# A hybrid encoder in fp32 halves: another simulation behind the scheduler's order

## The chip, the cores and the metric

The kernel runs on one core of one Trainium2 chip. The metric is the device time of one execution in microseconds (us), as the median of three runs. A profile of one further execution gives the instructions of each engine with their times. The engines are TensorE (PE in the profile, with its weight loads as PEld), VectorE (DVE), ScalarE (ACT), GpSimd (POOL) and SyncE (SP, which here only issues transfers).

## What is computed

Two layers of a bidirectional encoder over 512 tokens and 16 learned meta tokens (528 rows of 1024 channels). Each layer adds half a gated feed-forward block, a mixer of two parallel branches, and half a second feed-forward block:

```python
def reference(x, meta_tokens, norm_gains, ...):
    h = jnp.concatenate([meta, x], axis=1)
    for l in range(DEPTH):                      # DEPTH = 2
        h = h + 0.5 * swiglu(rmsnorm(h, norm_gains[l, 0]), ffn_w_gate[l, 0], ffn_w_up[l, 0], ffn_w_down[l, 0])
        h = h + mixer(rmsnorm(h, norm_gains[l, 1]), w_in[l], ...)
        h = h + 0.5 * swiglu(rmsnorm(h, norm_gains[l, 2]), ffn_w_gate[l, 1], ffn_w_up[l, 1], ffn_w_down[l, 1])
    return rmsnorm(h, final_norm)[:, N_META:]
```

The mixer projects to queries, keys, values and gates of both branches. Branch A is gated linear attention in both directions (4 heads), computed by chunks with a state carried from chunk to chunk. Branch B is softmax attention with 8 query heads and 2 key heads, normalised and rotated queries and keys. The branches are multiplied by sigmoid gates, added and projected back.

## The kernel before, in words

Channels lie on the 128 partitions and tokens along the free dimension; `h` is 8 chunks of 128 x 528. Every large product is made of three matmuls on halves: an operand is split into a high part `hi` (a cast, on ScalarE) and a low part `lo` (the difference, on VectorE), and hi*hi, hi*lo and lo*hi are summed in PSUM.

**Weights.** The class `Weights` goes through a plan (`PLAN`) of slabs of 128 x 1024. A slab is fetched by SyncE's queue (L168 and L203), cast to `whi` on ScalarE (L222) and subtracted to `wlo` on VectorE (L223), or on GpSimd while the gates are projected. `whi` and `wlo` have four buffers each and the raw slabs three. `use` makes slabs 4 places ahead (`AHEAD_MADE`) and fetches 6 ahead (`AHEAD_FETCHED`). The gate and up matrices of the feed-forward blocks are multiplied with seven products of sums of sub-blocks in place of eight; some of those sums of weights are formed by transfers that add into their target, issued on GpSimd's queue (L178), with a negated copy on ScalarE (L173) before them.

**Feed-forward blocks** (`ffn`). For each of 11 pairs of columns there are seven products (L498) of 24 matmuls; between them ScalarE copies partial results out of PSUM (`snap`, L504) and VectorE adds (L511, L516, L520, L531, L537). After each of three groups the down projection (`product`, L378) runs and is added to `h` (L465, L474). The last down product leads into the next norm: squares (L412), their sum (L416), the mean over channels as a matmul (`means`, L384), and the operands of the next stage (`Norm.pair`, L422 to L442, tiles `xc`, or `Norm.operand`, tiles `x`).

**Mixers** (`mixer`). Projections of x (`project`, L378 on the tiles `mm`) alternate in program order with the linear attention of two pairs of heads (`gla_pair`, L586 to L735: decays, transposes at L651, states at L687, scores inside a block at L714, outputs at L723 and L724) and with softmax attention (`attention`, L748 to L902: scores at L832 and L833, transposes of the probabilities at L857 and L867, weighted values at L874 and L875). One unit of attention is two blocks of 128 queries of one head; the probabilities of the next unit are made before the weighted values of this one. Four of the 16 gate projections come before attention in program order and twelve after it; none of them depends on attention.

**What sets the order.** The kernel is written in a framework that records instructions in program order, with their dependences and buffers, and orders them itself when the context is closed. For that it plays the program on a simulated machine: an engine of that machine is given, among the instructions whose inputs and buffers are ready in simulated time, the one of the highest priority. Priority is program order, except that `tc.high_priority()` raises what is recorded inside it (the mean of a norm in `Norm.rs`, the copies out of PSUM in `project`, the query norms in attention). `tc.issue_after` fixes an instruction behind another on the same engine. The result is one fixed stream per engine, DMA issues of SyncE, ScalarE and GpSimd among them, with waits on semaphores where another engine's work is needed. On the chip each engine executes its stream in that order, whatever is ready. By default the simulated machine is a simple one, which gives an engine its next instruction when the last one is over and starts each transfer after a fixed latency.

The diff touches only the line that opens the context, L1085 in `kernel`:

## Time and profile before

| what | us |
|---|---|
| median of 3 runs | 2314.39 (2314.13 to 2316.66) |
| the profiled execution | 2324.93 |
| its span, first to last instruction | 2323.2 |
| TensorE busy | 2244.2 |
| VectorE busy | 1525.0 |
| ScalarE busy | 1192.3 |
| GpSimd busy | 231.8 |

The mean clock granted to TensorE in the profiled execution is 0.983 of full speed. In the profile a row such as "PE ss L384 <- DVE t L416" says that PE's instruction of line 384, which writes the tile `ss`, stood still until VectorE's instruction of line 416 was over. L12 is line 12 of the kernel; a line can be that of a helper which many callers share, as L378 is. A wait for several things is put down to the last of them. A PE that is busy need not be at its peak: the records of matmuls overlap.

The stages follow each other in time as follows: first feed-forward block 0 to 400 us, mixer of layer 0 to 824, second feed-forward block to 1182, the first block of layer 1 to 1555, its mixer to 1961, the last block and the final norm to the end. In layer 1, from the mixer on, only the 512 tokens without the meta tokens are carried.

### The profile page before, as it was taken

The numbers are of one execution on the slowest core, as the hardware profiler recorded it, in microseconds if no ns is written. First come the engines' busy times: TensorE is split into PE (matmuls) and PEld (weight loads), VectorE is DVE, ScalarE is ACT, GpSimd is POOL, SyncE is SP. The second block draws the span as 40 slices with busy tenths as digits, with TensorE's granted clock in tenths as the row PEclk, the third lists the DMA queues.
The fourth block names the chain that finished last, engine by engine and source line by source line (L and its number), as shares of the span: only waits on it lengthen the run. The fifth ranks groups of instructions, "written<-read, shape, count | busy, mean of one in ns | idle before, by whom it ended". The sixth has DMA issues, their size and how long they took to land.

```text
span 2323.2 us, 39861 instructions
## 1 busy us (share of the span) xinstructions
PE 2244.2 (97%) x16548; PEld 2122.3 (91%) x16548; DVE 1525.0 (66%) x2355; ACT 1192.3 (51%) x1761; POOL 231.8 (10%) x218
## 2 busy tenths in 40 slices
PE   6999999999899999999989999999998999999997
PEld 5999999989899999999989999998787878989896
DVE  6657567566875676565676565674768767656666
ACT  7536354344784464453565353553446846636353
POOL 1111000000112010101011110100001110101010
PEclk9999999999998999999989999999999999999999
DMA  8868563111103386776658585632121135958671
GB/s 230 233 160 219 140 158 106 64 48 64 37 28 100 102 204 167 186 186 173 170 139 209 147 219 144 172 101 73 46 64 45 32 124 140 229 150 215 160 178 64
DMA packets 88412, 315.19 MB, mean 136 GB/s; under 512 B 9830, under 2 KB 12262, under 8 KB 88232
## 3 DMA queue, kind: packets, MB, share of 16 engines
q1 hardware_dynamic: 61136, 218.26, 28.4%
q0 software_dynamic: 25344, 92.29, 22.4%
q8 instruction: 130, 2.13, 0.4%
q10 hardware_dynamic: 1752, 2.11, 0.3%
q14 instruction: 50, 0.41, 0.1%
HBM read 264.38 MB, written 2.10 MB: 115 GB/s over the span
## 4 chain that ended last, share of the span: by engine, by line
PE 89%; DVE 6%; ACT 2%; issue 1%; DMA 1%; SPq 0%; DVEq 0%; POOL 0%; ACTq 0%
PE ss L498 38%; PE ss L378 27%; PE mm L378 12%; PE sm L378 3%; PE sm L857 1%; PE sm L874 1%; PE ss L714 1%; PE sm L875 1%; DVE wlo L223 1%; PE ss L832 1%; PE ss L384 1%; PE sm L687 1%; PE ss L833 1%; ACT whi L222 1%; PE sm L723 1%
## 5 line engine op out<-in xcount | busy, mean ns | idle before, releaser
L498 PE MATMUL ss<-xc,whi 128*128 128x264 f32 (+1 forms) x4928 | 902.3, 285 | 25.5 <-ACT whi L222 9.2
L498 PEld LDWEIGHTS ss<-xc,whi 128*128 128x128 f32 x4928 | 766.8, 189 | 28.1 <-ACT whi L222 9.9
L498 PE MATMUL ss<-xc,wlo 128*128 128x264 f32 (+1 forms) x2464 | 702.0, 285 | 3.5 <-DVE wlo L223 3.5
L378 PE MATMUL ss<-g,whi 128*128 128x264 f32 (+2 forms) x2668 | 494.2, 301 | 0.0
L498 PEld LDWEIGHTS ss<-xc,wlo 128*128 128x128 f32 x2464 | 466.0, 189 | 4.6 <-DVE wlo L223 4.4
L378 PEld LDWEIGHTS ss<-g,whi 128*128 128x128 f32 x2668 | 388.6, 188 | 17.4
L378 PE MATMUL mm<-x,whi 128*128 128x264 f32 (+1 forms) x1712 | 387.0, 318 | 0.1
L222 ACT CAST whi<-w 128x1024 fp32r<-128x1024 f32 (+1 forms) x221 | 230.8, 1047 | 257.9 <-PE ss L378 116.0
L222 ACT CAST whi<-raw 128x1024 fp32r<-128x1024 f32 x190 | 199.2, 1048 | 303.0 <-PE mm L378 108.0
L223 DVE TENSOR_TENSOR wlo<-w,whi 128x1024 fp32r<-128x1024 f32 (+1 forms) x221 | 267.9, 1218 | 108.5 <-ACT whi L222 106.3
L378 PE MATMUL ss<-g,wlo 128*128 128x264 f32 (+2 forms) x1334 | 310.0, 301 | 0.0
L378 PEld LDWEIGHTS mm<-x,whi 128*128 128x128 f32 x1712 | 283.3, 192 | 19.8 <-issue 2.5
L378 PE MATMUL mm<-x,wlo 128*128 128x264 f32 (+1 forms) x856 | 269.9, 320 | 0.0
L223 DVE TENSOR_TENSOR wlo<-raw,whi 128x1024 fp32r<-128x1024 f32 x166 | 203.1, 1224 | 98.6 <-ACT whi L222 97.5
L378 PEld LDWEIGHTS ss<-g,wlo 128*128 128x128 f32 x1334 | 213.4, 188 | 8.7
L223 DVE TENSOR_TENSOR wlo<-s,whi 128x1024 fp32r<-128x1024 f32 x88 | 107.6, 1223 | 101.7 <-ACT whi L222 101.7
L378 PEld LDWEIGHTS mm<-x,wlo 128*128 128x128 f32 x856 | 162.8, 192 | 11.0 <-issue 2.2
L222 ACT CAST whi<-s 128x1024 fp32r<-128x1024 f32 x88 | 92.4, 1050 | 154.1 <-PE ss L498 134.4
L465 DVE SCALAR_TENSOR_TENSOR t<-ss,rs 128x528 f32<-128x528 f32 (+1 forms) x95 | 66.0, 700 | 126.9 <-PE ss L378 126.8
L173 ACT ACTIVATE s<-w 128x1024 f32<-128x1024 f32 x88 | 93.3, 1060 | 84.6 <-DMA w<-win 47.9
L223 POOL TENSOR_TENSOR wlo<-raw,whi 128x1024 fp32r<-128x1024 f32 x24 | 57.7, 2403 | 363.0 <-ACT whi L222 279.7
L178 POOL DMA_DIRECT2D s<-win x44 | 41.1, 934 | 508.7 <-ACT s L173 508.4
(234 smaller groups left out, 2747.9 us busy)
## 6 DMA issues: line engine op xcount, KB each, us to landing
w<-win SPq DMA_DIRECT2D x219, 512.0 KB, 4.6
raw<-wts SPq DMA_DIRECT2D x190, 512.0 KB, 3.4
s<-win POOLq DMA_DIRECT2D x44, 512.0 KB, 6.8
w<-s POOLq DMA_DIRECT2D x44, 512.0 KB, 5.7
w<-win POOLq DMA_DIRECT2D x44, 512.0 KB, 6.9
s<-w POOLq DMA_DIRECT2D x44, 512.0 KB, 7.1
h<-xt SPq DMA_DIRECT2D x3, 528.0 KB, 6.6
out<-h SPq DMA_DIRECT2D x4, 256.0 KB, 2.3
```

What stands on the lines that cost most here:

```text
L173: self.nc.scalar.activation(t, w, AF.Copy, scale=-1.0)
L178: self.nc.gpsimd.dma_start(t, src, accum_op=ALU.add)
L222: nc.scalar.copy(hi[:, cs], w[:, cs])
L223: self.lo.tensor_tensor(lo[:, cs], w[:, cs], hi[:, cs].bitcast(F32), ALU.subtract)
L378: TE.matmul(acc.half[i][:width], lhs, rhs[:, acc.spans[i]], start=first, stop=last)
L384: TE.matmul(a, weights, x[:, hs], start=True, stop=True)
L465: V.scalar_tensor_tensor(cut(dst[rows]), pv[rows], -0.5 * f, cut(rs[rows]), ALU.mult, ALU.mult)
L498: TE.matmul(acc[:, j], a[:, j, k], b[:, at], start=bool(begin and k == 0 and i == 0), stop=k == len(x) - 1 and i == 2, skip_group_check=no ...
L687: TE.matmul(ps[:, hh * P : (hh + 1) * P], ktok(b, hh), vtok(b, hh), start=True, stop=True)
L714: TE.matmul(ats[:n, hh, d * n : (d + 1) * n], prods[d][1][rows, bs], prods[d][0][rows, bs], start=True, stop=True)
L723: TE.matmul(os_, vtok(b, hh), t3[:, hh], start=True, stop=False)
L832: TE.matmul(s[:n, i, :HF], lhs, kh[:, hs], start=True, stop=False)
```

## The change

The context is told to order the instructions by another simulated machine. It plays the whole program with a sequencer and a queue of issued instructions for each engine, with the queues and descriptor generation of the transfers, and with its own costs of instructions. Instructions, buffers, priorities, dependences and `issue_after` edges are what they were; the streams of all five engines and of the DMA queues are ordered anew.

```diff
-    with tile.TileContext(nc) as tc, ExitStack() as ctx:
+    with tile.TileContext(nc, schedule_with_timeline_sim=True) as tc, ExitStack() as ctx:
         build(tc, ctx, out=out, **aps)
```

## The prediction

> **What bounds the kernel now.** I read the page first: the span, the engines' busy time and the shares of the chain that ended last.
>
> ```profile
> span 2323.2 us, 39861 instructions
> PE 2244.2 (97%) x16548; PEld 2122.3 (91%) x16548; DVE 1525.0 (66%) x2355; ACT 1192.3 (51%) x1761; POOL 231.8 (10%) x218
> PEclk9999999999998999999989999999999999999999
> PE 89%; DVE 6%; ACT 2%; issue 1%; DMA 1%; SPq 0%; DVEq 0%; POOL 0%; ACTq 0%
> ```
>
> TensorE is busy in 2244.2 of 2323.2 us and holds 89% of the chain. A new order removes no instruction, so it can only touch the 79.0 us in which PE is idle and the stretches in which its clock is down (the two 8s among the slices of PEclk, and part of some 9s). The next question is where these lie, and the view of busy time by stretches answers it. I cut it at the feed-forward stages, the mixers, and the seams between them (columns: stretch, length, busy time of PE, PEld, DVE, ACT, POOL, then granted clock, DMA share and GB/s).
>
> ```profile
> 0.00:32.40 32.40, 10.79 (x51) 9.04 (x52) 24.73 (x49) 26.23 (x47) 3.85 (x8) 0.89 0.87 251
> 35.30:400.00 364.70, 364.70 (x2991) 364.46 (x2991) 230.90 (x291) 180.41 (x220) 34.10 (x39) 1.00 0.66 174
> 513.00:530.30 17.30, 17.30 (x69) 13.70 (x69) 6.85 (x22) 2.61 (x9) 0.00 (x0) 0.51 0.00 1
> 566.00:705.80 139.80, 132.42 (x998) 122.50 (x997) 109.35 (x260) 100.51 (x216) 19.27 (x8) 0.98 0.13 42
> 824.40:835.00 10.60, 9.20 (x72) 8.88 (x71) 8.78 (x17) 9.45 (x16) 1.72 (x2) 1.00 0.73 204
> 835.00:1182.20 347.20, 347.18 (x2852) 346.94 (x2850) 221.19 (x282) 175.46 (x216) 36.63 (x42) 1.00 0.72 180
> 1182.20:1199.30 17.10, 7.11 (x27) 6.40 (x28) 14.41 (x29) 10.80 (x20) 1.75 (x2) 0.60 0.55 121
> 1199.30:1555.00 355.70, 355.70 (x2903) 354.76 (x2903) 227.02 (x284) 175.67 (x213) 32.25 (x37) 1.00 0.65 165
> 1603.00:1700.00 97.00, 91.22 (x523) 73.03 (x522) 68.26 (x145) 42.74 (x86) 7.75 (x4) 0.95 0.16 50
> 1961.50:1970.00 8.50, 7.16 (x47) 6.12 (x46) 6.93 (x13) 7.09 (x12) 0.85 (x1) 1.00 0.79 229
> 1970.00:2306.70 336.70, 336.70 (x2360) 314.26 (x2358) 217.49 (x279) 164.99 (x202) 33.16 (x38) 1.00 0.67 168
> 2306.70:2323.30 16.60, 1.93 (x6) 0.65 (x4) 11.02 (x22) 3.33 (x8) 5.17 (x6) 0.66 0.37 126
> ```
>
> The four feed-forward stretches (364.70, 347.20, 355.70 and 336.70 us) have PE idle for 0.02 us together. The idle time is at the start (21.6 of 32.4 us), in the two seams at 824 and 1961 (1.4 and 1.3), the seam at 1182 (10.0), the end (14.7), and, with what is left, 79.0 - 49.0 = 30 us, in the two mixers. Who held PE there is in the list of waits of PE alone (us in total, times, longest).
>
> ```profile
> PE ss L651 <- DVE p L647: 11.8, 8, 2.0
> PE ss L498 <- ACT snap L504: 8.8, 1, 8.8
> PE ss L498 <- ACT xc L429: 7.3, 1, 7.3
> PE sm L857 <- DVE q L861: 6.6, 5, 2.0
> PE ss L384 <- DVE t L416: 5.4, 3, 2.7
> PE ss L832 <- DVE uq L806: 3.4, 2, 1.9
> PE ss L832 <- ACT t L361: 3.2, 4, 2.1
> PE ss L378 <- DVE x L367: 2.3, 1, 2.3
> PE sm L867 <- DVE e L881: 1.2, 2, 1.0
> PE sm L867 <- DVE sc L842: 0.9, 1, 0.9
> ```
>
> In the mixers the matmul that waits is always a step of the dependent chain (a transpose at L651, L857 or L867, scores at L832), while projections (L378) that need nothing from that chain stand later in PE's stream. PE takes its stream in order, so each of these waits says that the order had the chain step ready earlier than the chip did. That is the kind of error that another simulation changes.
>
> **The change part by part.** *Feed-forward stages: nothing.* The weights wait for PE there and not PE for the weights:
>
> ```profile
> ACT whi L222 <- PE ss L498: 342.7, 185, 6.2
> SPq L168 <- DVE wlo L223: 671.9, 178, 15.4
> s<-win POOLq DMA_DIRECT2D x44, 512.0 KB, 6.8
> 157.40 73.19 PE ss L498 x600
> L223 DVE TENSOR_TENSOR wlo<-w,whi 128x1024 fp32r<-128x1024 f32 x219 | 266.5, 1223 | 108.5 <-ACT whi L222 106.3
> ```
>
> The casts sit 342.7 us waiting for buffers that PE still reads, and SyncE's queue waits 671.9 us for buffers that the subtractions free. One matmul takes 73.19 / 600 = 0.122 us and a product of 24 takes 2.9, so the three other buffers of four cover 8.8 us. The changed order moves the DMA issues of SP and POOL too; an accumulating transfer that lands after 6.8 us still fits under that cover. If the cover went, a stall of 1 us in each of the 44 pairs of columns would cost 44 us; today the four stretches show none.
>
> *Start: a gain of 1.8 us.* PE's longest wait is on a copy:
>
> ```profile
> 27.46 1.04 ACT L222 CAST whi<-w 128x1024 fp32r<-128x1024 f32 x1 [1.09 <-DMA w<-s]
> 28.54 1.22 DVE L223 TENSOR_TENSOR wlo<-w,whi 128x1024 fp32r<-128x1024 f32 x1 [0.58 <-ACT whi L222]
> 29.94 1.05 ACT L222 CAST whi<-w 128x1024 fp32r<-128x1024 f32 x1 [1.43 <-DMA w<-win]
> 30.89 0.59 ACT L504 COPY snap<-ss 128x528 f32<-128x528 f32 x1
> 31.54 0.81 PE L498 MATMUL ss<-xc,whi 128*128 128x264 f32 x2 [8.83 <-ACT snap L504]
> ```
>
> The copy (0.59 us) stands on ScalarE behind two casts, the second of which waited 1.43 us for a transfer. An order that has the cast first must have taken that transfer for landed. With the copy first, PE could start when both halves of the first weight are there: whi at 28.50, wlo at 28.54 + 1.22 = 29.76, against 31.54. That is 1.8 us; by whi alone it would be 3.0, and 0 if the copy stays where it is. I take 1.8, because a third of that product needs wlo.
>
> *Mixers: a gain of 11.8 us.* The waits at L651, L857, L832, L867 and of L378 on x add up to 11.8 + 6.6 + 3.4 + 3.2 + 2.3 + 1.2 + 0.9 = 29.4 us, the top of the bound; the bottom is below zero (first rival). Something must run in place of the waiting step, and the chain in order of time shows that it is there: projections that run alone after attention.
>
> ```profile
> 705.77 21.92 PE mm L378 x159
> 1857.96 15.81 PE mm L378 x67
> ```
>
> I take L651 whole. It waits 8 times, once for each pair, direction and layer, for a product (L647) that follows a row of VectorE steps; an error that returns in the same place is one of the simulation. The other 17.6 us I leave: they fall on 16 of many like places, and removed ones will be replaced by others.
>
> *Seams: L384 gives 2.7 us, displaced steps cost 6.1.* The mean of the norms (L384) has raised priority and was put into PE's stream ahead of matmuls that could run; it waited 5.4 us in three seams. I take half, 2.7, the bounds being 0 and 5.4. Against it, at five places (start, 824, 1182, 1961, end) no work covers the chain of h, squares and operands, and every order is a new draw. One weight subtraction of 1.223 us set ahead of a chain step at each of the five costs 6.1 us; none costs 0, and the gain the same way is as large (the 7.3 us wait on xc holds such steps now). I take the cost: VectorE is busy 14.41 of the 17.10 us of the seam at 1182, so that a step added there lies on the path nearly wherever it is put.
>
> *Clock: a gain of 3.6 us.* From 513.00 to 530.30 PE was busy throughout at a clock of 0.51, with 69 small matmuls and hardly a projection between them: 17.30 x 0.49 = 8.5 us lost. In layer 1 the like work, in another order, had 0.95 over 97.00 us, which is 4.9 us lost. The difference, 3.6 us, is what another order of the same steps has been seen to be worth; the bounds are 8.5 and -8.5. [...]
>
> *Sum.* -1.8 - 11.8 - 2.7 + 6.1 - 3.6 = -13.8 us. The profiled execution took 2324.93 us, of which 1.73 lie outside its span; it would take 2311.1. The median of the runs, 2314.39, is 10.5 us (0.45%) below the profiled time, and the terms scaled by that stay the same within 0.1: 2314.4 - 13.7 = 2300.7, so 2301 us. Waits that are only half as curable, or displaced steps that are free, give its own range, 2289 to 2309.
>
> **The rivals.** *Slower: chain steps queue behind the projections.* The new simulation has queues: an engine's instruction is placed when it goes into the queue and not when the engine is free. A chain step that becomes ready then stands behind those already placed, and raised priority helps it less. In attention PE has two such steps in each unit, the transposes and the weighted products. These rows give the counts:
>
> ```profile
> L857 PE MATMUL sm<-const,t 128*128 128x128 f32 x256 | 42.1, 277 | 5.6 <-DVE q L861 5.4
> 412.63 23.28 PE mm L378 x192
> ```
>
> At 8 transposes a unit, 256 are 32 units, 16 a layer, so 32 steps a layer. A delay of d per step costs nothing while the projections left over (21.92 and 15.81 us) fill it: it decides from d = 0.68 us in layer 0 and 0.49 in layer 1. With 8 projection matmuls ahead (23.28 / 192 = 0.121 us each) d is 0.97 and the steps lose 31.0 us a layer, of which 9.1 and 15.2 remain: +24.3 us, 2339. For it: VectorE and ScalarE are busy only 109.35 and 100.51 of 139.80 us in attention, so latency and not throughput sets the pace. Against it: PE is already busy 132.42 of those 139.80 us, so delays of this size are there today and are absorbed. Chance 0.35, with times from 2320 up.
>
> *No change that can be measured.* About 0.2%, 4.6 us, is what a measurement of this kernel can tell from none. Where data force the order, both simulations give the same streams, and waits removed in one place come back in the next: 2310 to 2319, with 2314 in the middle. The case that the setting does nothing at all is in it. Chance 0.17.
>
> *Much faster.* All 29.4 us of the mixers, 5.4 of L384, 3.0 at the start and 8.5 of the clock: -46.3, so 2268. Against it: the projections would have to be dealt out over both mixers without running short. Chance 0.06.
>
> **How the numbers follow.** The forecast has 0.42. Faster by over 0.2% is 0.42 + 0.06 = 0.48, within it 0.17, slower 0.35. For 8 in 10 I go down to 2284, which leaves out the much faster case and a little of the forecast's edge (0.08), and up to 2342, just above the priced slower case, which leaves out about 0.11 of worse ones.
>
> **What the profile after would show.** The counts of instructions on PE stay at 16548, and the four feed-forward stretches keep their lengths within a microsecond; if they do not, the cover I leaned on was the thing that moved, and the forecast is wrong in kind. PE's waits at L651 on L647 should fall from 11.8 us to a few, and with them idle time between 446 and 566 and between 1603 and 1700. The copy at L504 should stand before the second cast at the start. The leftover stretch of L378 after attention should be shorter than 21.92 us; if it is gone and PE's idle time in attention has grown past 7.4 us, the slower rival is what happened. The clock should be near 1.00 around the second pair of the linear attention in layer 0; if instead the seam at 1182 has grown, the displaced steps were undersized.

## The result, and the profile after

The changed kernel took 2345.39 us (median; 2343.47 to 2349.27) beside 2315.52 us (2314.13 to 2320.17) of the kernel before: a ratio of 1.0116, with a 95% interval of 1.0091 to 1.0140. It is slower, and the forecast of 2301 us was wrong in sign. The traces show less of the difference than the medians do (24.0 us of span against 29.9 us), mainly because the execution of before that was profiled took 2324.93 us, 9.4 above this median, at a granted clock of 0.983 (0.981 to 0.989 in the executions of it beside the experiments). The page of the changed kernel's profiled execution (2349.27 us) begins so:

```profile
span 2347.2 us, 39938 instructions
PE 2244.8 (96%) x16548; PEld 2124.0 (90%) x16548; DVE 1523.7 (65%) x2355; ACT 1187.7 (51%) x1761; POOL 233.3 (10%) x218
```

PE is busy as long as before (2244.8 against 2244.2 us), with as many matmuls. Of the 24.0 us of span, 23.4 are idle time of PE: 102.4 us in place of 79.0. Where it lies, the busy time by stretches shows. I cut both traces where the same work starts: at the runs of 600 matmuls of L498 in the middle of a feed-forward block, and at the run of projections that opens each mixer. The columns are: stretch, length, busy time of PE, PEld, DVE, ACT and POOL, granted clock, DMA share and GB/s. The rows are: start; rest of the first block; mixer of layer 0 and half a block; two halves of blocks; mixer of layer 1 and half a block; end. First before, then after:

```profile
0.00:157.40 157.40, 135.79 (x1062) 133.63 (x1063) 100.79 (x144) 87.94 (x121) 18.73 (x25) 0.97 0.79 211
157.40:412.63 255.23, 255.23 (x2095) 254.37 (x2094) 161.63 (x204) 126.08 (x154) 20.10 (x23) 1.00 0.59 155
412.63:957.29 544.66, 527.37 (x4078) 505.32 (x4077) 362.14 (x675) 282.94 (x502) 54.34 (x37) 0.97 0.34 95
957.29:1579.89 622.60, 612.51 (x4905) 606.03 (x4905) 398.93 (x515) 315.21 (x393) 58.45 (x67) 0.99 0.66 166
1579.89:2089.92 510.03, 494.63 (x2885) 419.53 (x2885) 349.42 (x615) 272.40 (x458) 54.93 (x37) 0.99 0.36 101
2089.92:2323.20 233.28, 218.71 (x1535) 203.46 (x1533) 152.13 (x204) 107.77 (x136) 25.25 (x29) 0.98 0.60 154
```

```profile
0.00:155.45 155.45, 138.14 (x1062) 134.78 (x1063) 100.03 (x144) 87.84 (x121) 18.69 (x25) 0.98 0.81 214
155.45:410.38 254.93, 254.93 (x2094) 254.18 (x2094) 160.46 (x204) 125.87 (x154) 20.07 (x23) 1.00 0.59 156
410.38:958.85 548.47, 523.11 (x4077) 503.76 (x4077) 362.95 (x675) 282.09 (x502) 56.81 (x37) 0.97 0.34 94
958.85:1580.53 621.68, 611.62 (x4906) 605.30 (x4905) 396.24 (x515) 313.73 (x393) 58.43 (x67) 0.99 0.65 166
1580.53:2113.94 533.41, 498.32 (x2885) 422.58 (x2885) 352.54 (x615) 270.61 (x458) 53.84 (x37) 0.97 0.35 97
2113.94:2347.20 233.26, 218.69 (x1535) 203.40 (x1533) 151.44 (x204) 107.58 (x136) 25.43 (x29) 0.97 0.60 154
```

Everything outside the mixers is where it was within 1 us, or 2 us better (the start). The stretch of the mixer of layer 0 grew by 3.8 us: its idle time of PE grew by 8.1 (548.47 - 523.11 = 25.4 against 17.3) and its busy time fell by 4.3. That of layer 1 grew by 23.4 us, of which 19.7 are idle time of PE (533.41 - 498.32 = 35.1 against 510.03 - 494.63 = 15.4). Who held PE (the waits of PE in the trace after: total, times, longest):

```profile
PE ss L498 <- ACT whi L222: 18.9, 6, 7.2
PE ss L651 <- DVE p L647: 16.2, 3, 5.7
PE ss L832 <- ACT t L361: 15.0, 15, 1.2
PE ss L498 <- ACT xc L429: 10.6, 4, 8.3
PE sm L867 <- DVE e L881: 9.4, 9, 5.7
PE sm L857 <- DVE q L861: 6.2, 7, 1.3
```

L651 was to fall and rose from 11.8 to 16.2 us, now in three long waits in place of eight short ones. In the timeline these three end at 466.86, 1636.52 and 1710.55 us (5.68, 5.63 and 4.86 us long), in the linear attention, while projections that need nothing from it still stand later in PE's stream: the next ones start at 469.25, 1638.92 and 1712.94 us, and the last cast and subtraction of a weight ahead of them were over at 462.6, 1632.4 and 1706.4 us. L832 on ScalarE went from 3.2 to 15.0; those waits are in attention, where few projections are left to run. What the chain itself met is seen in the timeline of the linear attention in layer 1, from the first state product (L687) of the first pair to its first output (L723). The PE rows of before, and then of after (a few of the rows between), each with the row of VectorE that makes the score block for this output:

```profile
1633.74 0.71 PE L687 MATMUL sm<-k 16*128 16x128 f32 x4
1634.38 0.71 PE L687 MATMUL sm<-q,q 128*128 128x128 f32 x4
...
1637.93 0.71 PE L714 MATMUL ss<-p,p 64*128 64x128 f32 x6
1638.58 0.49 PE L723 MATMUL sm<-t,q 128*128 128x128 f32 x2
1634.34 0.45 DVE L718 COPY_PREDICATED t<-mask,ss 128x256 f32<-128x256 uint32 x1
```

```profile
1643.42 0.71 PE L687 MATMUL sm<-k 16*128 16x128 f32 x4
...
1646.92 0.60 PE L687 MATMUL sm<-q,q 128*128 128x128 f32 x4
1647.29 0.48 PE L378 MATMUL mm<-x,wlo 128*128 128x512 f32 x1
...
1652.83 0.63 PE L378 MATMUL mm<-x,whi 128*128 128x512 f32 x2
1653.30 0.40 PE L378 MATMUL mm<-x,wlo 128*128 128x512 f32 x1
1653.53 0.63 PE L378 MATMUL mm<-x,whi 128*128 128x512 f32 x2
...
1654.93 0.38 PE L723 MATMUL sm<-t,q 128*128 128x128 f32 x2
1639.50 0.44 DVE L718 COPY_PREDICATED t<-mask,ss 128x256 f32<-128x256 uint32 x1
```

Before, the chain's matmuls stand one behind the other, 4.84 us from the first to the output. After, 29 projection matmuls stand between them (L378 on `mm`, counted in the timeline), at 1653.53 - 1652.83 = 0.70 us for three, so 6.8 us, and the same way takes 11.51 us. After, the score block for this output (L718 on VectorE) was over at 1639.94 us, 15 us before L723 began; before, it was over 3.8 us ahead.

What that does to the mixer of layer 1 is told by two lines, each with the time of its first and last start: the softmax of attention (L840) and the copies of the gate projections (L578). Before, then after:

```profile
L840 DVE TENSOR_TENSOR sc<-sc,rq x32: 127/150/2314, 1738.3 to 1842.4; 128x1 f32<-128x1 f32 x32
L578 ACT COPY g<-mm x16: 557/585/593, 1656.8 to 1874.4; 128x512 f32<-128x512 f32 x16
```

```profile
L840 DVE TENSOR_TENSOR sc<-sc,rq x32: 128/159/161, 1781.2 to 1882.9; 128x1 f32<-128x1 f32 x32
L578 ACT COPY g<-mm x16: 572/586/596, 1648.6 to 1822.4; 128x512 f32<-128x512 f32 x16
```

The mixers start within 0.7 us of each other (1579.89 and 1580.53). Attention starts 43 us later after the change, and the gates are done 52 us earlier. Before, gates last until 136 us after attention has begun, longer than its 104 us of softmax; after, they last for 41 us. The rest of attention stands alone. Two rounds of it from the timeline of after, then the busy time from the last gate to the end of attention:

```profile
1849.01 0.38 PE L867 MATMUL sm<-const,t 128*16 128x128 f32 x2
1850.63 0.39 PE L832 MATMUL ss<-k,p 128*128 128x264 f32 x1 [1.24 <-ACT t L361]
...
1854.15 0.38 PE L867 MATMUL sm<-const,t 128*16 128x128 f32 x2
1855.77 0.39 PE L832 MATMUL ss<-k,p 128*128 128x264 f32 x1 [1.24 <-ACT t L361]
```

```profile
1822.00:1915.00 93.00, 77.29 (x451) 61.93 (x451) 64.75 (x154) 65.94 (x139) 0.90 (x1) 0.95 0.10 29
```

The first fence repeats every 5.14 us, with PE idle for 1.24 us at the first scores of the next unit, which wait for ScalarE. In all PE is idle for 15.7 of these 93 us (5.7 of them in one wait of L867), of the 35.1 in the whole stretch of the mixer.

### The profile page after: what moved, and what is told of

The parts are those of the page before. It is cut to its first block, busy times and chain, and to the rows that moved or that the text cites. A ratio compares the mean times of both kernels' runs of the same rounds, so it can differ in the third digit from the quotient of the medians.

```text
span 2347.2 us, 39938 instructions
## 1 busy us (share of the span) xinstructions
PE 2244.8 (96%) x16548; PEld 2124.0 (90%) x16548; DVE 1523.7 (65%) x2355; ACT 1187.7 (51%) x1761; POOL 233.3 (10%) x218
## 4 chain that ended last, share of the span: by engine, by line
PE 86%; DVE 7%; ACT 4%; DMA 2%; issue 1%; DVEq 0%; ACTq 0%
PE ss L498 37%; PE ss L378 25%; PE mm L378 14%; PE sm L378 3%; PE sm L874 1%; PE sm L857 1%; PE sm L875 1%; DVE g L951 1%; ACT whi L222 1%; PE ss L832 1%; DVE wlo L223 1%; DMA w<-s 1%; ACT t L361 1%; PE ss L714 1%; PE ss L833 1%
## 5 line engine op out<-in xcount | busy, mean ns | idle before, releaser
L498 PE MATMUL ss<-xc,whi 128*128 128x264 f32 (+1 forms) x4928 | 905.2, 286 | 30.2 <-ACT whi L222 18.9
L498 PEld LDWEIGHTS ss<-xc,whi 128*128 128x128 f32 x4928 | 766.0, 190 | 36.4 <-ACT whi L222 20.7
L498 PE MATMUL ss<-xc,wlo 128*128 128x264 f32 (+1 forms) x2464 | 693.4, 285 | 0.7 <-DVE wlo L223 0.7
L378 PE MATMUL ss<-g,whi 128*128 128x264 f32 (+2 forms) x2668 | 495.1, 301 | 0.0
L498 PEld LDWEIGHTS ss<-xc,wlo 128*128 128x128 f32 x2464 | 463.7, 190 | 1.5 <-DVE wlo L223 1.3
L378 PEld LDWEIGHTS ss<-g,whi 128*128 128x128 f32 x2668 | 388.8, 188 | 16.9
L378 PE MATMUL mm<-x,whi 128*128 128x264 f32 (+1 forms) x1712 | 386.4, 318 | 3.8 <-ACT x L366 2.0
L378 PE MATMUL ss<-g,wlo 128*128 128x264 f32 (+2 forms) x1334 | 310.0, 301 | 0.0
L378 PEld LDWEIGHTS mm<-x,whi 128*128 128x128 f32 x1712 | 284.0, 192 | 27.5 <-ACT x L366 2.7
L378 PE MATMUL mm<-x,wlo 128*128 128x264 f32 (+1 forms) x856 | 267.7, 316 | 0.0
L378 PEld LDWEIGHTS ss<-g,wlo 128*128 128x128 f32 x1334 | 213.4, 188 | 8.6
L378 PEld LDWEIGHTS mm<-x,wlo 128*128 128x128 f32 x856 | 163.0, 192 | 10.1 <-issue 1.3
```

The lines of the kernel that those rows point to most:

```text
L378: TE.matmul(acc.half[i][:width], lhs, rhs[:, acc.spans[i]], start=first, stop=last)
L498: TE.matmul(acc[:, j], a[:, j, k], b[:, at], start=bool(begin and k == 0 and i == 0), stop=k == len(x) - 1 and i == 2, skip_group_check=no ...
```

## The experiments

**Theory (A):** the new simulated machine places an instruction when it enters an engine's simulated queue, and for PE this queue is set to hold 35. Projections are ready early and fill it; a step of the chain that becomes ready goes behind them. So the chain is late by up to a queue of projections at each step, the projections run out sooner, and attention is left uncovered. **Rivals:** (B) the simulated queues of the other engines, set to 12, do it, by displacing chain steps on VectorE and ScalarE; (C) the new machine's costs and transfers give a worse order, whatever the queues.

**One change of size: the window of PE.** The scheduler's machine takes the length of its queues from a table. In the kernel after, and only while it is scheduled, PE's entry in that table is set to 2; the other engines' entries stay. All these numbers are settings of the simulated machine; how long the chip's own queues are, no run shows.

> The changed kernel, with one number of the new simulation altered: TensorE's window of issued instructions is 2 in place of 35; the other engines keep 12. Theory A (the window: a chain step that becomes ready is placed behind all projections that already sit in PE's window, so the chain is late and the projections run out before attention ends): the wait from L718 to L723, which grew from 2.8 and 2.1 us to 8.2 and 12.4 us in layers 0 and 1, falls under 5; the kernel is back within 10 us of the kernel before, 2305 to 2325 us. Theory B (the windows of VectorE and ScalarE: casts and subtractions of weights and the early scaling of gates, L951, stand ahead of the chain): nothing of this changes, 2340 to 2350 us.

With 70 in place of 2:

> The changed kernel with the suspected cause doubled: TensorE's window is 70 in place of 35. In the order that comes out, 42 projection matmuls are left for the attention of layer 1 in place of 135 (the kernel before has 221); layer 0 is unchanged. Theory A: 93 matmuls fewer at 0.233 us leave 21.7 us more of attention uncovered, 2355 to 2375 us, all of it in the mixer of layer 1. Theory B: 2340 to 2350 us.

With 8, and with 1:

> The changed kernel with TensorE's window at 8. The order has 276 projection matmuls in the attention of layer 1 and 543 in layer 0. Theory A: between the 2 and the 35, near the 2: 2295 to 2310 us, with the wait from L718 to L723 a little over that of window 2 (1.2 us a block in layer 0, 2.1 to 2.3 in layer 1) and far under 8.

> The changed kernel with TensorE's window at 1. The order now errs the other way: chain steps are placed first, but only 18 and 25 projection matmuls run beside attention in layers 0 and 1 and 399 and 299 stand behind it. If attention without projections beside it is what costs, and not the lateness of the chain as such, this is slow as well, near the kernel with all gates early (2371 us): 2350 to 2385 us. If only lateness of the chain costs: 2285 to 2300 us.

And with 16:

> A PE window of 16, between 8 (2299 us) and 35 (2345). Theory (the lateness of each step of the chain grows with the window, and part of it is covered by projections that are left): between the two, 2305 to 2335 us. Rival (the loss comes with one reordering that happens at or above some size and not by degrees): within 5 us of either end.

Each was timed beside the kernel before, whose median was 2315.52 to 2320.36 us in these series; the ratios are to the median of the same series. "Wait for PE" is the time from the end of L718 on VectorE to the start of its L723 on PE, the mean over the 10 blocks of layer 0 and the 8 of layer 1 in the timeline; "gates in attention" is the time from the first start of L840 to the last of L578 in layer 1, as read above.

| kernel | us | ratio to before (95%) | wait for PE, layer 0 / 1 | gates in attention |
|---|---|---|---|---|
| before | 2315.52 | 1 | 2.8 / 2.1 | 136 |
| window 1 | 2651.11 | 1.1432 (1.1403 to 1.1461) | 0.5 / 0.7 | 196 |
| window 2 | 2295.01 | 0.9901 (0.9882 to 0.9921) | 2.2 / 2.3 | 128 |
| window 8 | 2298.64 | 0.9922 (0.9905 to 0.9939) | 3.0 / 4.2 | 108 |
| window 16 | 2308.58 | 0.9945 (0.9928 to 0.9963) | 4.6 / 6.1 | 80 |
| window 35 (after) | 2345.39 | 1.0116 (1.0091 to 1.0140) | 8.15 / 12.4 | 41 |
| window 70 | 2401.27 | 1.0358 (1.0335 to 1.0381) | 13.0 / 20.2 | 4 |

(The expectation for 8 gives the wait with a window of 2 as 1.2 us in layer 0; the mean over the 10 blocks is 2.2.) From 2 to 70 the wait grows with the window at every step, the cover of attention shrinks, and the time follows. With nothing changed but this number, the change's sign turns: C falls. Up to 16 the longer wait costs little; that projections are left to pay with (80 us of cover) fits this. Two results lie outside the ranges that (A) gave. A window of 2 was to be back at 2305 to 2325 us and came out below the kernel before. A window of 70 was to take 2355 to 2375 us, with all of the loss in the mixer of layer 1, and took 2401. Its span is 51.7 us longer than after: the stretch of layer 0's mixer, which was to stay as it was, grew by 31.0 us, and what follows it by 21.4, near the 21.7 that were expected of layer 1:

```profile
409.70:989.15 579.45, 535.73 (x4078) 512.28 (x4077) 368.23 (x675) 281.34 (x502) 53.67 (x37) 0.93 0.32 89
```

The cover in layer 0 hardly shrank (82 us after, 74 with 70), so the lost cover of attention isn't all that a long window costs: PE's waits at L651 alone are 39.0 us, 17.5 of them in layer 0, where after the change there were 5.7.

With a window of 2, the waits of PE at L651 and the two mixer stretches, cut as above, are:

```profile
PE ss L651 <- DVE p L647: 1.8, 4, 0.7
```

```profile
409.31:940.10 530.79, 515.73 (x4077) 497.02 (x4077) 361.06 (x675) 281.11 (x502) 54.29 (x37) 0.99 0.35 97
1563.29:2059.63 496.34, 487.34 (x2886) 418.07 (x2885) 345.98 (x615) 271.40 (x458) 53.74 (x37) 1.00 0.37 103
```

Against before, the mixers are 13.9 and 13.7 us shorter: 8.6 us of idle time (15.06 + 9.00 against 17.29 + 15.40) and 18.9 us of busy time for the same matmuls, at a granted clock of 0.99 and 1.00 in place of 0.97 and 0.99. Not all of this busy time is the order's: the run with edges under the default simulation (below), which has nearly the waits of before, has 4.8 us less in these two stretches than the profiled one of before. That leaves some 14 us.

A window of 1 was a miss in size: I had expected some per cent and it cost 14. Part of the why is in its waits:

```profile
PE ss L384 <- DVE t L416: 46.0, 6, 11.6
PE ss L651 <- DVE p L647: 42.2, 8, 6.7
PE sm L867 <- DVE q L861: 29.0, 18, 3.6
PE sm L857 <- DVE e L881: 22.8, 18, 4.6
```

Its order has the chain first everywhere. Gates are left over in plenty (196 us from the first softmax to the last gate), but PE stands at a step of the chain that is not ready and may not take the projection behind it. The rest is busy time: 2380.6 us for the same 16548 matmuls in place of 2244.2, at a granted clock of 0.92 in place of 0.983. Of the 315.8 us by which the span grew, 136.4 are that, and 179.4 idle time. So a short queue alone is not what is good; the best of the sizes that were run are 2 and 8, which their intervals do not tell apart.

**The other engines' windows.** VectorE, ScalarE, GpSimd and SyncE at 2 in place of 12 in the same table, PE at 35:

> The changed kernel with the windows of VectorE, ScalarE, GpSimd and SyncE at 2 in place of 12, TensorE's window at 35 as it was. Theory A: 2340 to 2350 us, 138 projection matmuls in the attention of layer 1 as before this edit (135). Theory B: back towards the kernel before, 2310 to 2325 us.

2351.72 us, ratio 1.0150 (1.0128 to 1.0172), just above the range of (A): as slow as after, with the wait for PE at 8.4 / 11.9 us and the same waits at L651 (16.0 us in 3) and L832 (15.8 us in 15). B falls. With all windows at 2 together, the best kernel of the study:

> The changed kernel with the windows of all engines at 2: run 1 (2295 us) and run 3 together. Since the other engines' windows did nothing at TensorE's 35, theory A expects what TensorE's 2 gave, 2288 to 2302 us. If the windows of VectorE and ScalarE cost something that TensorE's hid: under 2285 us.

2292.51 us, ratio 0.9894 (0.9878 to 0.9910). The interval overlaps that of PE's window alone, so the other windows are worth nothing that was measured in either kernel.

**What an uncovered attention costs.** The kernel before, with its default simulation, but all 16 gate projections ahead of attention in program order:

```diff
-EARLY = 4
+EARLY = 16
...
-        gates = [project(x, None, "g", n=n_out) for _ in range(EARLY)]
+        gates = [project(x, None, "g", n=n_out) for _ in range(4)]
+        W.lo = G
+        gates += [project(x, None, "g", n=n_out) for _ in range(EARLY - 4)]
+        W.lo = V
         bt = attention(l, x, rs, n_out)
-        W.lo = G
-        gates += [project(x, None, "g", n=n_out) for _ in range(2 * KC - EARLY)]
-        W.lo = V
```

(`EARLY` also places the gates' slabs in `PLAN`. The low parts of these twelve gates are made on GpSimd, as they were.)

> The kernel before, default simulation, with all 16 gate projections in program order ahead of attention (EARLY = 16) in place of 4, so that no projection is left to run beside attention whatever the simulation. Same work. Theory A needs that attention without projections is dear: after the change a unit without them takes 5.15 us, of which PE idles 1.45, so 16 units cost 23 us a layer and the prologue some more: 2360 to 2420 us. If projections beside attention are not what matters (theory B): 2310 to 2330 us.

2371.45 us, ratio 1.0236 (1.0217 to 1.0256). The same wait as after the change leads its list, and larger:

```profile
PE ss L832 <- ACT t L361: 27.7, 18, 5.7
```

The chain is on time here (the wait for PE is 1.7 and 2.1 us). So the lack of cover by itself costs more than the change did, with no new simulation in it.

**Holding the gates back.** If the missing gates were the whole cause, tying them to attention would be the cure. In the kernel after, ten of the twelve later gate projections are each fixed behind a unit of attention (unit k - 2), the first two behind attention's first scores (the lines that collect `units_done` and `qk_first` are left out here):

```diff
-        gates += [project(x, None, "g", n=n_out) for _ in range(2 * KC - EARLY)]
+        for k in range(2 * KC - EARLY):
+            with after(units_done[k - 2] if k > 1 else qk_first[0]):
+                gates.append(project(x, None, "g", n=n_out))
```

> The changed kernel, simulation untouched (TensorE's window 35). In the source, twelve issue_after edges on TensorE keep the twelve later gate projections behind attention's first scores and then one behind each unit of attention. No wait on another engine and no work is added. In the order that comes out, 285 projection matmuls fall into the attention of layer 1 (changed kernel 135, kernel before 221) and 588 into that of layer 0 (444 and 405). Theory A (TensorE's window lets the projections run ahead and they are missing later): most of the loss of 30 us is gone, 2295 to 2325 us, although the window is as wide as in the changed kernel. If the width did harm in another way than through the projections: over 2335 us.

2369.36 us, ratio 1.0223 (1.0205 to 1.0242): a miss, slower than after. The waits of PE (L836 here is L832 of the other kernels, L823 and L787 make queries and keys):

```profile
PE ss L651 <- DVE p L647: 16.2, 3, 5.7
PE ss L836 <- DVE p L823: 9.5, 1, 9.5
PE ss L836 <- ACT k L787: 5.4, 1, 5.4
```

L651 waits exactly as in the kernel after, and the wait for PE is still 8.1 and 9.1 us: the linear attention is late with the twelve gates held back too, so other projections stand before its steps. Which ones, I did not separate. With the gates held back, PE stands 9.5 us for the first scores of layer 0 and 5.4 us for those of layer 1. The gates then do run beside attention (the last is copied 127.6 us after the first softmax), and yet the softmaxes of layer 1 stretch over 139 us, against 102 in the kernel after. To separate the edges from the late chain, I ran the same edges with PE's window at 2 and under the default simulation:

> The edges that hold twelve gate projections behind units of attention, together with a PE window of 2 in the scheduler's simulated machine (all else as in the kernel after). Theory (the window of 35 makes the chain of the linear attention late, and the held gates could not mend that): with the chain on time the held gates cost nothing, so the time is that of the window of 2 alone, 2290 to 2305 us, PE's waits at L651 are under 4 us, and there is no PE idle of over 3 us at a wait on L823 in layer 1. Rival (the edges cost by themselves, whatever the window: a held projection may not fill an idle PE ahead of its unit): 2320 us or more, with the waits on L823 and L787 of the run with the edges alone still there.

> The same twelve edges under the default simulation (the kernel before with the edges added). If the edges cost by themselves, this is slower than the kernel before by 10 us or more (2325 up); if only the late chain made them dear, it is within 10 us of the kernel before, 2305 to 2325 us.

With the window at 2: 2303.70 us, ratio 0.9933 (0.9912 to 0.9954). Under the default simulation: 2320.97, ratio 1.0004 (0.9987 to 1.0021). So the edges cost nothing under the default order, at most some tenths of a per cent with a window of 2 (0.9933 against 0.9901, intervals that overlap), and about 1% with 35. They are dear only where the chain is late. The missing gates are a consequence; the window is the cause of the loss.

## Why the prediction was wrong, step by step

**The step that failed** is the mixers' gain of 11.8 us, with the weight given to the first rival. In place of the gain the two mixer stretches grew by 27.2 us (3.8 and 23.4), and the waits at L651, all of which I had taken as curable, rose from 11.8 to 16.2. The reading "another simulation changes the error at L651" held: with a window of 2 the waits fall to 1.8 us. What I did not weigh enough is that the new machine brings an error of its own, in the other direction: before, PE stood at a step that was not ready; after, a step that was ready stood behind projections, and PE stood longer. My argument against the rival was that "delays of this size are there today and are absorbed". They were not there: the wait for PE was 2.8 and 2.1 us and became 8.15 and 12.4. What absorbs them is the stock of projections, and in layer 1 it was used up 41 us after the first softmax.

**The rival, priced at +24.3 us,** was the mechanism, and the total came out near it (+26.8 by the ratio on 2314.39), but by luck. I took 8 matmuls ahead of each of 32 steps of attention in each layer. In fact some 29 stood between one pair's steps, and the delay that counted was collected in the linear attention, before attention began: from the start of the mixer of layer 1 to the first softmax it took 200.7 us in place of 158.4, while the softmaxes themselves took 101.7 in place of 104.1. The split is other than priced, too: +3.8 and +23.4 us for layers 0 and 1, against 9.1 and 15.2. And the price of a matmul was wrong for layer 1: by the leftover row there, 15.81 / 67 = 0.236 us and not 0.121, the same sum would have given 9.1 + 44.6 = 53.7 us. I set the point from which it decides by the leftover stretches (21.92 and 15.81 us), and they are gone after the change, as the sign I had named.

Two slips in the working change nothing in this: the other 17.6 us of mixer waits fall on 15 places by their list, not 16, and the lower edge of 2289 comes out only if the displaced steps are a gain of 6.1 us, while free ones give 2295.

**Start, -1.8:** right. The copy came ahead of the casts, and PE's long wait ended at 28.84 us in place of 31.54, on the cast of a weight (`whi`) and no longer on the copy:

```profile
24.35 0.57 ACT L504 COPY snap<-ss 128x528 f32<-128x528 f32 x1
24.83 1.70 ACT L412 ACTIVATE t<-h 128x528 f32<-128x528 f32 x3
27.74 2.94 ACT L222 CAST whi<-w 128x1024 fp32r<-128x1024 f32 x3 [1.21 <-DMA w<-s]
```

The next landmark is 1.95 us earlier. **L384, -2.7:** its waits on L416 went from 5.4 to 0.5 us, but the seam at 1182, where most idle time of that kind lies, is no shorter: the fourth row of the two tables of stretches has 10.1 us of idle time in both. PE waits there for the next operand instead (xc at L429, 10.6 us in all in place of 7.3). **Displaced steps, +6.1:** nothing of the kind is to be seen. The seam at 1182 and the end (14.6 us idle in both) are as they were, the start is shorter, and PE's waits in the seams behind the two mixers are 2.0 us each in place of 1.4 and 1.3. I had taken one end of a range for want of a reason. **Feed-forward stages:** nothing, as forecast. The second row differs by 0.3 us.

**Clock, -3.6:** the stretch at 513 us is gone (the clock is 1.00 from 500 to 535 us after), but others came, and the mixers' granted clock is 0.97 and 0.97 after, against 0.97 and 0.99 before. Some of them stand at PE's longest waits: with waits of 5.68, 5.63, 4.86 and 5.73 us that end at 466.86, 1636.52, 1710.55 and 1822.62 us, the clock is 0.60, 0.50, 0.50 and 0.61 in the 5 us from 465, 1635, 1710 and 1820 us; before, no wait in the mixers is longer than 2.3 us. With a window of 2 the clock is 0.99 and 1.00, and the mixers' busy time is 18.9 us shorter (14 beside the other run named above), where my bound was 8.5. So a redrawn order can move busy time by more than idle time (8.6 us there).

Left open: why a long window costs what it costs in each place (I changed its length, and not the choice of what goes into it), and what part of the edges' 1% at 35 is the hole ahead of attention and what part the slower units in it.

## What to carry to other kernels

A list scheduler with a queue commits ready work before urgent work; where independent filler is plentiful early and short late, look for how far ahead the scheduler commits, and sweep it, before judging its cost model. The stock of filler left when the dependent stage begins (here the gates after the first softmax: 128, 108, 80, 41 and 4 us) goes with the time from a window of 2 to one of 70, as does the mean wait for PE. It does not order all the kernels: the kernel before has more of it than the window of 2 and is slower, and a window of 1 leaves 196 us and is the slowest. And an edge that saves filler for later helps only if the chain that is to use it is on time.

## What the runs showed of the hardware

The same matmuls of the second pair of the linear attention of layer 0, which ran at a clock of 0.51 before (513.00 to 530.30, 69 matmuls), ran at full clock with a window of 2, with 128 matmuls in as long a stretch, projections between the chain's:

```profile
511.00:528.00 17.00, 17.00 (x128) 14.18 (x128) 10.75 (x31) 4.57 (x15) 0.00 (x0) 1.00 0.10 32
```

PE is busy throughout in both. What sets the clock there isn't shown: before, a gap of 1.66 us stands ahead of the slow stretch, at transposes of that pair (L651), and with a window of 2 the same transposes follow the projections without one.

```profile
511.46 0.63 PE L651 MATMUL ss<-const,p 128*128 128x128 f32 x4 [1.66 <-DVE p L647]
```

Over the whole program PE's busy time went from 2244.2 us before to 2226.0 with a window of 2, for the same 16548 matmuls; in the run with edges under the default simulation it was 2239.1.
